# Repricing a planner's reductions and narrow matmuls, and splitting one weight blob a stage earlier, in a decoder layer

## The chip, the cores and the metric

The kernel runs on one core of one Trainium2 chip. The metric is device microseconds of one execution, from the runtime's measurement around the program; the profile's span, from the first to the last instruction, is 1.8 us shorter. A core has TensorE (PE: matmuls, with its weight loads PEld), VectorE (DVE), ScalarE (ACT), GpSimd (POOL) and SyncE (SP, which here only issues loads). Each runs its own instructions in the order in which they are written.

## The reference

One layer of a hybrid decoder for 512 tokens of width 2048, all in float32. Cut to what matters here:

```python
mod = silu(c) @ W_ada + b_ada            # shift1, scale1, gate1, shift2, scale2, gate2
h   = modulate(rms_norm(x), shift1, scale1)
u   = h @ W_in                           # conv group | 8 query heads | k, v of 3 branches | gates
y_conv = B * causal_conv3(C * H)         # 1024 channels
y_nsa  = attention(...)                  # 8 heads of 128, 2 kv heads; blocks of 128 queries
x   = x + gate1 * ([rms_norm(y_conv) | rms_norm(y_nsa)] @ W_out)
h   = modulate(rms_norm(x), shift2, scale2)
x   = x + gate2 * (relu(h @ W1) ** 2 @ W2)
out = rms_norm(x)
```

For each block of 128 queries, attention has a compressed branch (32 columns of pooled keys), a selected branch and a sliding-window branch. With 512 tokens every block of keys is selected, so that the last two are plain causal softmax over the keys so far. The three results are weighted by sigmoid gates and added.

## The kernel before

Matmuls keep float32's precision by splitting each operand into a high half and a low half (both F32R) and adding three products: high by high, high by low, low by high (`mm3`). A weight blob of 128 x 1024 is loaded by SP into a buffer `raw` (three of them, numbered 115 to 117 here), ScalarE rounds it to the high half, and VectorE subtracts to get the low half (`weights`). Both halves lie in a pair named `wh` in the profile (two pairs, 113 and 114).

The kernel has three stages, each recorded in full and then ordered by a planner (`Order`) before anything is issued:

- the front stage: the adaLN products (`wa`, dotted with silu(c) on VectorE into `late` and summed into `mod`), the projections of h (`ps`), compression, convolution, and the convolution half normalised into `mix`;
- the attention stage: for two groups of four heads and four blocks of 128 queries, scores (`s`, three PSUM banks), their maximum (`nm`) on VectorE, the exponential (`p`) on ScalarE, scaling by gate over sum (`cf`), transposes of p through TensorE (`pt`, two banks), the split of each transpose into `tt` (high half ScalarE, low half VectorE) and the product with the values (`pv`); `sr` is the sum of squares at the end of a block. Beside these, out_conv(m), m from 0 to 15, multiplies blob m of `w_oc` by `mix`: 24 matmuls into `pw`, 384 in all, ended by an update of `x` on VectorE. Nothing in attention waits for them; they are what TensorE does while it waits. Four query heads of the second group get their rotary embedding (`rt`, `t`, `q`) here too;
- the feed-forward stage: the attention half of the output projection, then the two large products.

The planner replays a recorded stage with a price for each instruction (`price`: duration, and a lag until its result is seen), a queue for each engine, bandwidth for loads and a count of buffers. At every step it takes the instruction that can start first, and among equals the one with the lower lane number, then the one wanted first. Lanes 0 to 2 order TensorE's work: what has lane 0 (transposes and pv) stands ahead of scores (1) and of out_conv (2). Where TensorE would wait in the replay, it takes the next lane. It makes six passes, each with the last one's times as targets, and keeps the shortest. What comes out is written as the program order of every engine, so that at run time an engine never takes a later instruction first: a price that is wrong is not corrected on the chip.

`with wanted()` gives what is recorded in it a target `SOON` (10 us) ahead of the end of the stage, as against 10 us behind it for work that nothing in the stage needs. Tiles that the next stage reads are kept.

Of the kernel before, what the change touches and what calls it, by code (L numbers as in the profile page):

```python
# [48 lines left out]
class Order:  # L49
# [43 lines left out]
    def price(self, eng, op, out, ins, kw):  # L93

        n = Order.width(out)
        if "dma" in op:
            return (0.42 if eng == "sync" else 0.55), 0.0
        if eng == "tensor":
            if op == "matmul" and ins[0].dtype == F32:
                return max(self.wide[0], n * self.wide[1]), 0.2  # L100
            return (0.109 if op == "transpose" else max(0.06, 0.0015 + n * 0.000453)), 0.2
        if eng == "scalar":
            aps = len(ins) - 1
            more = 0.1 if kw.get("accum_out") is not None else 0.0
            return (0.18 if n < 16 else 0.09 + 0.00084 * n + (0.09 * max(0, aps) if not more else 0.19)), 0.16
        if n < 16:
            return 0.1, 0.14
        if op == "scalar_tensor_tensor":
            return 0.14 + 0.00101 * n, 0.14
        if op in ("tensor_scalar", "tensor_copy", "memset"):  # L110
            return 0.13 + 0.0005 * n, 0.14
        if op == "tensor_reduce":
            n = max(Order.width(x) for x in ins) * (1.7 if n > 16 else 1)
        return 0.068 + 0.00104 * n, 0.14

    def record(self, eng, op, real, args, kw):
# [159 lines left out]
def hybrid_layer(ctx: ExitStack, tc: tile.TileContext, a, out):  # L276
# [91 lines left out]
    def weights(src, cols=1024, spare=False):  # L368
        raw = next(wraw)[:, :cols]
        nc.sync.dma_start(out=raw, in_=src)  # L370
        wh, wl = (slot(F32R, name="sw") for _ in range(2)) if spare else next(whl)
        wh, wl = wh[:, :cols], wl[:, :cols]
        nc.scalar.activation(wh, raw, AF.Copy)
        nc.vector.tensor_tensor(out=wl, in0=raw, in1=wh.bitcast(F32), op=OP.subtract)
        return wh, wl
# [123 lines left out]
    def scale_col(which, k, sc, g, n=1):  # L499
        nc.vector.scalar_tensor_tensor(out=aff[:, which * NK + k:which * NK + k + n],  # L500
                                       in0=mod[:, sc * NK + k:sc * NK + k + n], scalar=1.0,
                                       in1=vec[:, g + k:g + k + n], op0=OP.add, op1=OP.mult)
# [145 lines left out]
    for s, (name, k) in enumerate(steps[:-1]):  # L648
        grp = 0 if name == "w_kv" else 1
        first, last = (grp, k) in begins, (grp, k) in finals  # L650
        if first:
            ps = [bank() for _ in range(8)]
        wh, wl = w
# [168 lines left out]
    for j in range(8):  # L822
# [4 lines left out]
        for i in range(3):  # L827
            n = 3 * j + i
# [30 lines left out]
    for g in range(NG):  # L859
        pv = [bank() for _ in range(NQ)]  # L860
        for blk in range(4):
            wh, wl = weights(a["w_v"][g * 4 + blk], BLOB)
# [49 lines left out]
    for g in range(NG):  # L912
        pq = [bank() for _ in range(NR)]
        order_k = range(NK) if g < NG - 1 else range(NK - 1, -1, -1)
        for at, k in enumerate(order_k):
            if at % 2 == 0:
                wh, wl = weights(a["w_q"][g * 8 + k // 2])
# [13 lines left out]
        tick()  # L931
    more_ada(len(todo))
    scale_col(1, 0, M_SC2, V_N2, NK)
    for t in [rot] + qs + raws + kwin + list(vv.values()) + mix:
        order.keep(t)
    order.emit()
# [25 lines left out]
    def out_conv(m):  # L962
        if m % 2 == 0:
            x1.append(pair(name="x1"))
            order.keep(x1[-1])
            nc.sync.dma_start(out=x1[-1], in_=a["xt"][m // 2])
        ps = next(pws)
        wh, wl = weights(a["w_oc"][m])
        with lane(2):
            for k in range(8):  # L970
                s = slice(k * P, (k + 1) * P)
                mm3(ps, wh[:, s], wl[:, s], mix[k][:, 0], mix[k][:, 1], k == 0, k == 7)
        x = x1[m // 2][:, m % 2]
        nc.vector.scalar_tensor_tensor(out=x, in0=ps, scalar=col(M_G1, m), in1=x, op0=OP.mult, op1=OP.add)
# [90 lines left out]
    m = 2  # L1065
# [111 lines left out]
    for k in range(8):  # L1177
        wh, wl = oa[k] if k < 2 else hilo(hl_tile(), raw_blob(a["w_oa"][k]))
# [315 lines left out]
    for f in range(8):  # L1494
# [7 lines left out]
        for q in range(3 if last else 4):  # L1502
            raw = [raw_blob(a["w_f2"][4 * f + q, b]) for b in range(4)]
            ps = [{}, {}]
            for i, w in enumerate(operands(raw, 4 * f + q)):
# [3 lines left out]
                for j in range(2):  # L1509
                    mp = 2 * q + j  # L1510
                    m = 2 * mp
# [119 lines left out]
```

## Time and profile before

| what | value |
|---|---|
| three runs | 2114.53, 2115.92, 2116.34 us (median 2115.92) |
| the profiled execution | 2115.59 us, span 2113.8 us |
| busy share of the span | PE 98%, weight loads 91%, DVE 89%, ACT 48%, POOL 6% |
| granted TensorE clock, mean | 0.993 |
| attention stage | 554.25 to 759.2 us |
| maxima of scores (nm) | 64, on 128 to 512 columns |
| DMA | 454 MB, 215 GB/s |

A line of the profile's groups gives engine, operation, the tile written and those read, shapes and count, then busy time and mean duration in ns, then the engine's idle time just ahead and who ended it. All recorded operations have one line of code, 122, that of the planner's record; so rows are told apart by their tiles. A line of the order in time gives start, duration, engine, operation and count; matmuls are pipelined, so their durations overlap, and what one costs is read from the starts of a run of them.

### The profile page before, as it was taken

The numbers are of one execution on the slowest core, as the hardware profiler recorded it, in microseconds if no ns is written. First come the engines' busy times: TensorE is split into PE (matmuls) and PEld (weight loads), VectorE is DVE, ScalarE is ACT, GpSimd is POOL, SyncE is SP. The second block draws the span as 40 slices with busy tenths as digits, with TensorE's granted clock in tenths as the row PEclk, the third lists the DMA queues.
The fourth block names the chain that finished last, engine by engine and source line by source line (L and its number), as shares of the span: only waits on it lengthen the run. The fifth ranks groups of instructions, "written<-read, shape, count | busy, mean of one in ns | idle before, by whom it ended". The sixth has DMA issues, their size and how long they took to land.

```text
span 2113.8 us, 38166 instructions
## 1 busy us (share of the span) xinstructions
PE 2068.4 (98%) x15070; PEld 1923.7 (91%) x15070; DVE 1885.7 (89%) x3039; ACT 1007.3 (48%) x1471; POOL 128.2 (6%) x244
## 2 busy tenths in 40 slices
PE   8999999999999999999999999999999999999997
PEld 6888787898777779999999999999999999999997
DVE  7999888888987556999999999999899999999997
ACT  5432433222455434766666666666444333334354
POOL 0000000000000001022211112111000000000000
PEclk8999999999999999999999999999999999999998
DMA  8897588888321144467666676668976466476442
GB/s 335 340 340 249 181 297 325 315 288 311 138 80 41 51 141 154 135 215 225 210 204 207 207 217 200 208 206 288 332 268 211 167 242 220 145 255 237 150 172 90
DMA packets 144130, 454.17 MB, mean 215 GB/s; under 512 B 15824, under 2 KB 20176, under 8 KB 143952
## 3 DMA queue, kind: packets, MB, share of 16 engines
q1 hardware_dynamic: 108816, 386.72, 53.0%
q0 software_dynamic: 34048, 63.98, 9.6%
q8 instruction: 118, 1.93, 0.4%
q10 hardware_dynamic: 1088, 1.05, 0.1%
q14 instruction: 60, 0.49, 0.1%
HBM read 383.53 MB, written 68.16 MB: 214 GB/s over the span
## 4 chain that ended last, share of the span: by engine, by line
PE 72%; DVE 9%; DMA 4%; ACT 2%; issue 2%; DVEq 0%; POOL 0%; SPq 0%; ACTq 0%
PE pf L122 55%; PE ps L122 11%; PE pw L122 3%; DMA rw<-in_w_f 1%; PE pv L122 1%; DVE hl L122 1%; DVE t L122 1%; DVE x L122 1%; PE s L122 1%; DMA wa<-in_w_ada 1%; PE pt L122 1%; DMA raw<-in_cmp_w 1%; DVE nm L122 1%; DVE wh L122 1%; DMA tk<-g 1%
## 5 line engine op out<-in xcount | busy, mean ns | idle before, releaser
L122 PE MATMUL pf<-tk,hl 128*128 128x256 f32 x10704 | 1223.3, 277 | 3.0 <-DVE hl L122 2.2
L122 PEld LDWEIGHTS pf<-tk,hl 128*128 128x128 f32 x10704 | 1219.9, 188 | 5.3 <-DVE hl L122 3.5
L122 ACT ACTIVATE hl<-rw 128x1024 fp32r<-128x1024 f32 x269 | 285.5, 1062 | 324.9 <-PE pf L122 280.1
L122 DVE TENSOR_TENSOR hl<-rw,hl 128x1024 fp32r<-128x1024 f32 (+2 forms) x351 | 336.5, 968 | 29.4 <-ACT hl L122 29.2
L122 ACT ACTIVATE hl<-sg 128x1024 fp32r<-128x1024 f32 x180 | 191.1, 1062 | 220.3 <-PE pf L122 172.8
L122 PE MATMUL ps<-h_m,wh 128*128 128x512 f32 x1080 | 252.0, 390 | 0.0
L122 DVE SCALAR_TENSOR_TENSOR t<-wa,cs 128x1024 bf16<-128x1024 f32 x192 | 234.5, 1221 | 16.1 <-DMA wa<-in_w_ada 13.8
L122 PEld LDWEIGHTS ps<-h_m,wh 128*128 128x128 f32 x1080 | 201.1, 188 | 41.5 <-DVE wh L122 0.3
L122 ACT ACTIVATE wh<-raw 128x1024 fp32r<-128x1024 f32 (+1 forms) x106 | 112.7, 1063 | 243.8 <-PE ps L122 215.7
L122 DVE TENSOR_TENSOR hl<-sg,hl 128x1024 fp32r<-128x1024 f32 (+2 forms) x193 | 188.1, 986 | 25.3 <-ACT hl L122 25.3
L122 PE MATMUL ps<-h,wh 128*128 128x512 f32 x840 | 198.7, 392 | 3.4 <-ACT h L122 2.3
L122 PEld LDWEIGHTS ps<-h,wh 128*128 128x128 f32 x840 | 157.7, 189 | 37.0 <-ACT h L122 2.7
L122 DVE TENSOR_TENSOR wh<-raw,wh 128x1024 fp32r<-128x1024 f32 (+1 forms) x106 | 129.9, 1225 | 21.2 <-ACT wh L122 19.9
L122 DVE TENSOR_TENSOR sg<-sg,rw 128x1024 f32<-128x1024 f32 x120 | 146.1, 1217 | 0.2
L122 DVE SCALAR_TENSOR_TENSOR x<-pf,mod,x 128x256 f32<-128x256 f32 (+1 forms) x280 | 131.8, 485 | 14.5 <-PE pf L122 12.8
L122 POOL DMA_DIRECT2D g<-gt x192 | 101.2, 532 | 379.7 <-ACT hl L122 222.1
L122 PE MATMUL pw<-mix,wh 128*128 128x512 f32 x384 | 109.7, 405 | 0.0
L122 DVE TENSOR_TENSOR sg<-rw 128x1024 f32<-128x1024 f32 x60 | 73.2, 1220 | 16.7 <-DMA rw<-in_w_f 14.0
L122 ACT ACTIVATE t<-t 128x512 f32<-128x512 f32 (+3 forms) x131 | 74.9, 572 | 21.1 <-DVE t L122 18.8
L122 PEld LDWEIGHTS pw<-mix,wh 128*128 128x128 f32 x384 | 69.6, 190 | 11.0 <-issue 0.5
L122 DVE TENSOR_TENSOR rw<-rw 128x1024 f32<-128x1024 f32 x60 | 73.0, 1217 | 0.0
L122 ACT ACTIVATE gt<-t 128x512 fp32r<-128x512 f32 x96 | 60.3, 630 | 22.6 <-DVE t L122 17.7
(215 smaller groups left out, 1802.1 us busy)
## 6 DMA issues: line engine op xcount, KB each, us to landing
rw<-in_w_f SPq DMA_DIRECT2D x263, 512.0 KB, 3.9
wa<-in_w_ada SPq DMA_DIRECT2D x192, 512.0 KB, 6.0
tk<-g SPq DMA_DIRECT2D x114, 512.0 KB, 6.2
g<-gt POOLq DMA_DIRECT2D x192, 256.0 KB, 4.1
raw<-in_w_conv SPq DMA_DIRECT2D x32, 512.0 KB, 4.3
x<-in_xt SPq DMA_DIRECT2D x16, 512.0 KB, 7.2
raw<-in_w_kv SPq DMA_DIRECT2D x16, 512.0 KB, 4.4
raw<-in_w_cv SPq DMA_DIRECT2D x16, 512.0 KB, 4.5
```

The costliest lines, as they stand in the source:

```text
L122: x.i, x.eng, x.call = len(self.nodes), eng, (lambda: real(*args, **kw))
```

## The change

Two edits. In `price`: a reduction on VectorE (`tensor_reduce`) is priced by the columns that it reads, also where it writes fewer than 16; before, such a one fell under the rule for small outputs, 0.1 us. A maximum over 512 scores goes from 0.1 to 0.60 us in the plan, one over 128 from 0.1 to 0.20. A matmul of F32R operands costs at least 0.1 us in the plan instead of 0.06; this touches those of 32, 128 and 160 columns, all of them scores or their masks. In `hybrid_layer`: the first blob of `w_oc` is loaded and split at the end of the front stage, as wanted, and out_conv(0) uses it.

```diff
         if eng == "tensor":
             if op == "matmul" and ins[0].dtype == F32:
                 return max(self.wide[0], n * self.wide[1]), 0.2
-            return (0.109 if op == "transpose" else max(0.06, 0.0015 + n * 0.000453)), 0.2
+            return (0.109 if op == "transpose" else max(0.1, 0.0015 + n * 0.000453)), 0.2
...
+        if op == "tensor_reduce":
+            rows = max(Order.width(x) for x in ins)
+            return 0.068 + 0.00104 * rows * (1.7 if n > 16 else 1), 0.14
         if n < 16:
             return 0.1, 0.14
...
-        if op == "tensor_reduce":
-            n = max(Order.width(x) for x in ins) * (1.7 if n > 16 else 1)
         return 0.068 + 0.00104 * n, 0.14
...
     scale_col(1, 0, M_SC2, V_N2, NK)
+    with wanted():
+        first = [weights(a["w_oc"][0])]
     for t in [rot] + qs + raws + kwin + list(vv.values()) + mix:
         order.keep(t)
     order.emit()
...
         ps = next(pws)
-        wh, wl = weights(a["w_oc"][m])
+        wh, wl = first.pop() if first else weights(a["w_oc"][m])
         with lane(2):
```

Every engine has the same instructions before and after; what differs is their order. The feed-forward stage keeps its order, and so does the front stage, but for the moved blob. In attention most of the order is new. Rows before have L122, rows after L123 (three lines more).

First place: TensorE where attention begins, behind the third group of scores (`kslc`: the selected branch with its compressed columns, `kwin`: the window, `vec`: the identity of the transposes). Before:

```order
L122 MATMUL s<-kslc_108,q 128x160 x2
L122 MATMUL s<-kwin,q 128x128
L122 MATMUL s<-mask_r,ident_r 128x128
L122 MATMUL s<-kwin,q 128x128 x3
L122 MATMUL s<-mask_r,ident_r 128x128
L122 MATMUL s<-kwin,q 128x128 x3
L122 MATMUL s<-mask_r,ident_r 128x128
L122 MATMUL s<-kwin,q 128x128 x2
L122 MATMUL pt<-vec,p 128x128 x2
L122 MATMUL pw<-mix,wh 128x512
```

These begin with the fourth group's last two; up to the first pair of transposes there is no `pw`. After, from the third group on:

```order
L123 MATMUL s<-kslc_108,q 128x160 x2
L123 MATMUL pw<-mix,wh 128x512 x3
L123 MATMUL s<-kslc_108,q 128x160
L123 MATMUL s<-mask_r,ident_r 128x128
L123 MATMUL s<-kslc_108,q 128x160 x2
L123 MATMUL pw<-mix,wh 128x512 x2
L123 MATMUL s<-kwin,q 128x128
L123 MATMUL s<-mask_r,ident_r 128x128
L123 MATMUL s<-kwin,q 128x128 x3
L123 MATMUL s<-mask_r,ident_r 128x128
L123 MATMUL s<-kwin,q 128x128 x2
L123 MATMUL pw<-mix,wh 128x512 x2
```

Out_conv's matmuls have moved between the scores: 3, 2, 2, and then (not shown) 4 and 1 ahead of the first transpose. Up to the end of the first block (its `sr`) 35 of the 384 stand now, 20 before; up to the second's 54 and 47; behind the row norm's broadcast at the end of attention (`pt<-t,ones`) 70 and 77.

Second place: VectorE at the end of the front stage, where the adaLN dots end and `mod` is summed. Before:

```order
L122 TENSOR_TENSOR wh_114<-raw_116,wh_114 128x1024
L122 SCALAR_TENSOR_TENSOR t_101,late_138<-wa_133,cs_127 128x1024
L122 SCALAR_TENSOR_TENSOR t_101,late_138<-wa_130,cs_126 128x1024
L122 SCALAR_TENSOR_TENSOR t_101,late_138<-wa_131,cs_127 128x1024
L122 SCALAR_TENSOR_TENSOR t_101,late_138<-wa_132,cs_126 128x1024
L122 SCALAR_TENSOR_TENSOR t_101,late_138<-wa_133,cs_127 128x1024
L122 TENSOR_TENSOR mod_124<-late_138 128x16
```

And after:

```order
L123 TENSOR_TENSOR wh_114<-raw_116,wh_114 128x1024
L123 SCALAR_TENSOR_TENSOR t_101,late_138<-wa_133,cs_127 128x1024
L123 SCALAR_TENSOR_TENSOR t_101,late_138<-wa_130,cs_126 128x1024
L123 TENSOR_TENSOR wh_113<-raw_117,wh_113 128x1024
L123 SCALAR_TENSOR_TENSOR t_101,late_138<-wa_131,cs_127 128x1024
L123 SCALAR_TENSOR_TENSOR t_101,late_138<-wa_132,cs_126 128x1024
L123 SCALAR_TENSOR_TENSOR t_101,late_138<-wa_133,cs_127 128x1024
L123 TENSOR_TENSOR mod_124<-late_138 128x16
```

The blob's low half has moved three dots ahead of the sum. On ScalarE its high half (wh_113 from raw_117) stands behind that of wh_114 and ahead of the four copies of `ps`; on SP its load stands four adaLN loads earlier, behind that of the last blob of w_q and one adaLN load.

Third place: VectorE in the third block of the first group, from the split of the compressed branch's transpose to that of the window's first one. Before:

```order
L122 TENSOR_TENSOR tt_3987<-pt_3975,tt_3987 128x512
L122 TENSOR_REDUCE nm_3993<-s_3972 128x1
L122 TENSOR_SCALAR p_3978<-p_3978,cf_4000 128x512
L122 TENSOR_REDUCE nm_3993<-s_3973 128x1
L122 TENSOR_SCALAR p_3979<-p_3979,cf_4000 128x512
L122 TENSOR_SCALAR p_3980<-p_3980,cf_4000 128x512
L122 TENSOR_REDUCE nm_3993<-s_3971 128x1
L122 TENSOR_TENSOR tt_3985<-pt_3974,tt_3985 128x512
```

And after:

```order
L123 TENSOR_TENSOR tt_3990<-pt_3978,tt_3990 128x512
L123 TENSOR_REDUCE nm_3996<-s_3975 128x1
L123 TENSOR_REDUCE nm_3996<-s_3976 128x1
L123 RECIPROCAL cf_4003<-sm_3999 128x4
L123 MEMSET pc_3991 128x96
L123 TENSOR_TENSOR cf_4003<-cf_4003,gates_241 128x4
L123 TENSOR_SCALAR p_3980<-p_3980,cf_4003 128x512
L123 TENSOR_TENSOR tt_3988<-pt_3977,tt_3988 128x512
```

The third maximum and two of the scalings of the next block now stand behind the split. On TensorE, between the first of the three `pv` matmuls that read this `tt` and the other two, which need VectorE's half, three `pw` stand instead of two. The rotary pieces of the second group have moved later: 10 of the 20 stand ahead of the second block's `sr`, where 15 did.

## The prediction

> **What bounds the kernel now.** I read the page first, then the busy time by stages, then the waits of TensorE, then the order of time at the one place where they pile up. TensorE bounds nearly everywhere:
>
> ```profile
> span 2113.8 us, 38166 instructions
> ...
> PE 2068.4 (98%) x15070; PEld 1923.7 (91%) x15070; DVE 1885.7 (89%) x3039; ACT 1007.3 (48%) x1471; POOL 128.2 (6%) x244
> ```
>
> The change can act only in the attention stage, 554.25 us (first score matmul) to 759.2 us (last out-projection matmul of the conv half); the order before 554 us differs in one moved blob, and the order of the feed-forward stage is the same instruction for instruction. The next rows (stretch, then busy us of PE, PEld, DVE, ACT, POOL, then TensorE's granted clock) show the stage, and five neighbouring stretches at its start:
>
> ```profile
> 554.25:600.00 45.75, 41.48 (x216) 33.33 (x215) 41.72 (x126) 26.02 (x78) 0.00 (x0) 0.93 0.24 86
> 554.25:759.20 204.95, 197.38 (x1019) 156.40 (x1018) 156.83 (x381) 101.37 (x258) 0.00 (x0) 0.98 0.20 66
> ...
> 553.09:556.51 3.42, 2.63 (x18) 2.24 (x16) 2.68 (x10) 1.80 (x3) 0.00 (x0) 1.00 1.02 413
> 556.51:559.92 3.41, 2.32 (x16) 2.01 (x16) 3.30 (x12) 2.31 (x9) 0.00 (x0) 1.00 0.62 253
> 559.92:563.33 3.41, 2.67 (x12) 2.34 (x11) 2.75 (x10) 2.01 (x8) 0.00 (x0) 0.50 0.03 7
> 563.33:566.75 3.42, 3.42 (x14) 3.14 (x13) 2.79 (x10) 2.73 (x8) 0.00 (x0) 0.50 0.49 153
> 566.75:570.16 3.41, 3.41 (x24) 3.15 (x24) 3.02 (x12) 1.02 (x5) 0.00 (x0) 1.00 0.11 13
> ```
>
> Two losses are to be seen. TensorE is idle for 204.95 - 197.38 = 7.6 us of the stage, and from 559.92 to 566.75 us it runs at half clock. All that the stage loses by name is in TensorE's own list of waits (total us, times, longest):
>
> ```profile
> PE pv L122 <- DVE tt L122: 4.3, 8, 0.7
> PE s L122 <- ACT p L122: 1.8, 2, 1.4
> PE pt L122 <- DVE p L122: 0.7, 1, 0.7
> PE pt L122 <- DVE sr L122: 0.2, 1, 0.2
> ```
>
> That is 7.0 us. The three waits of the second and third row, 2.5 us, stand in the first block of attention, just ahead of the half clock (start, duration, count, and in brackets the idle time before and its releaser):
>
> ```profile
> 554.77 0.27 PE L122 MATMUL s<-mask_r,ident_r 128*128 128x128 f32 x1
> ...
> 555.32 0.40 PE L122 MATMUL s<-kslc,q 128*128 128x160 f32 x2
> 557.07 0.34 PE L122 MATMUL s<-kslc,q 128*128 128x160 f32 x1 [1.35 <-ACT p L122]
> ...
> 558.17 0.33 PE L122 MATMUL s<-kwin,q 128*128 128x128 f32 x1 [0.42 <-ACT p L122]
> ...
> 560.79 0.69 PE L122 MATMUL pt<-vec,p 128*128 128x128 f32 x2 [0.74 <-DVE p L122]
> 561.14 0.78 PE L122 MATMUL pw<-mix,wh 128*128 128x512 f32 x1
> ...
> 741.32 18.06 PE L122 MATMUL pw<-mix,wh 128*128 128x512 f32 x77
> ```
>
> TensorE fills its three score banks by 555.7 us and then has nothing: no out-projection matmul (pw) stands in its order until 561.14 us, since in the old plan the first blob of w_oc is split only then. (The last row, from the end of the stage, gives the price of a pw in a dense run: 18.06 / 77 = 0.235 us.)
>
> **The change, part by part.** *What the new prices tell the planner.* Measured reductions against what they were priced at:
>
> ```profile
> L122 DVE TENSOR_REDUCE nm<-s 128x1 f32<-128x512 f32 x16 | 11.0, 685 | 1.2 <-PE s L122 1.2
> ...
> L122 DVE TENSOR_REDUCE nm<-s 128x1 f32<-128x128 f32 x16 | 4.2, 280 | 0.9 <-PE s L122 0.8
> ```
>
> The old rule gave 0.1 us to each; the new one gives 0.068 + 0.00104 x 512 = 0.60 and 0.20. Over 64 maxima (16 of each width, prices 0.20, 0.33, 0.47, 0.60) that is 16 x 1.2 = 19 us of VectorE's 156.8 us that the old plan did not see. So it planned VectorE early where it was late. The price of narrow matmuls (0.06 to 0.10) moves toward what the trace shows: from 554.77 us the mask matmul and the three narrow ones after it run to the next mask at one per 0.11 us. No instruction is added or removed on any engine; all is order.
>
> *Term 1, the first block.* The new order puts pw matmuls between the scores: 3 after the third score, then 2, 2, 4 and 1, twelve ahead of the first transposes (the order shown above, first place). Of the 1.35 us wait, 3 x 0.235 = 0.7 is filled; the rest stays, because the fourth score needs the first maximum and its exponential, and these do not come sooner:
>
> ```profile
> 535.02 1.22 DVE L122 TENSOR_TENSOR wh<-raw,wh 128x1024 fp32r<-128x1024 f32 x1
> ...
> 548.73 1.23 DVE L122 SCALAR_TENSOR_TENSOR t<-wa,cs 128x1024 bf16<-128x1024 f32 x1
> ...
> 553.76 1.23 DVE L122 SCALAR_TENSOR_TENSOR t<-wa,cs 128x1024 bf16<-128x1024 f32 x1 [1.26 <-DMA wa<-in_w_ada]
> ...
> 555.55 0.63 DVE L122 TENSOR_TENSOR rt<-qr,rot 128x512 f32<-128x512 f32 x1
> 556.09 0.28 DVE L122 TENSOR_REDUCE nm<-s 128x1 f32<-128x128 f32 x1
> ...
> 556.38 0.68 DVE L122 TENSOR_TENSOR rt<-qr,rot 128x512 f32<-128x512 f32 x1
> ...
> 556.56 0.37 ACT L122 ACTIVATE p<-s,nm 128x128 f32<-128x128 f32 x1 [1.51 <-DVE pc L122]
> ```
>
> VectorE's queue up to that maximum (adaLN dots, then one rope piece at 555.55, then the maximum at 556.09) is the same in both orders. The 0.42 us is covered by two pw (0.47). The 0.74 us goes, since the transposes now stand behind twelve pw and a ninth group of scores; a split of the second blob (1.22 us) stands ahead of the four scalings on VectorE in the new order, which I allow 0.2 us. Left: 0.65 + 0.25 = 0.9 of 2.5 us. Gain 1.6 (bounds 0.7, if only the first wait shrinks, and 2.5).
>
> *Term 2, the clock.* In the half-clock stretch TensorE was busy 2.67 + 3.42 = 6.09 us; at full clock that work takes half. Gain 3.05 if the clock is kept, 0 if not. The stretch ahead of the drop was 68% busy (2.32 of 3.41); the one before that, 77% (2.63 of 3.42), kept the clock. With at most 0.75 us idle the new first stretch is 78% or more, and its filling is 512 columns wide. So I take 3.05.
>
> The Trainium skill, "TensorE: Matmul & The Clock Gate", section "Part 1: The HAM clock gate (the "warmup" mystery)", has the clock halved after an idle window of about 3.4 us, and under "HAM oscillation" warns only of gaps beyond that. The trace agrees with the window's length (half clock for 6.83 us, twice 3.41) but not with the condition, since the longest gap here was 1.35 us. By that rule these gaps are not what decides, and the sum would be 3.05 us less; that is the first rival.
>
> *Term 3, the later waits,* 4.3 + 0.2 = 4.5 us, nine of them, each where a pair of pv matmuls waits for VectorE's half of a split transpose (tt). The one at 616.58 us:
>
> ```profile
> 614.26 0.60 ACT L122 ACTIVATE tt<-pt 128x512 fp32r<-128x512 f32 x1 [2.36 <-PE pt L122]
> ...
> 615.24 0.68 DVE L122 TENSOR_REDUCE nm<-s 128x1 f32<-128x512 f32 x1
> 615.84 0.68 DVE L122 TENSOR_TENSOR tt<-pt,tt 128x512 fp32r<-128x512 f32 x1
> ...
> 616.58 0.73 PE L122 MATMUL pv<-tt,vv 128*128 128x512 f32 x2 [0.67 <-DVE tt L122]
> ```
>
> ScalarE's half is done at 614.86, but the split stands in VectorE's queue behind three maxima, planned at 0.1 us each and taking 0.6. In the new order (third place above) two maxima and one scaling (and three operations on four or 96 columns) stand between it and the split ahead of it, where three and three stood, and TensorE has three pw instead of two ahead of the pair: at least the one maximum, 0.6 us, less queue and 0.23 us more cover, against 0.67. I read the other places only by their pw counts, so I take just over half: gain 2.5. Bounds: +4.5, and -1.0, two new waits of about 0.5 from the heavier rope work behind the second block.
>
> *Term 4, the blob moved into the front stage.* Its load is one place in SP's queue ahead of four adaLN loads and waits for its buffer until VectorE's split of 535.02 us ends, 536.2; the load behind it feeds the dot at 548.73 or later, 12 us on. ScalarE's half has to wait until TensorE frees the operand buffer, one blob (24 matmuls, 5.6 us at 0.23) before 554.25, at 548.7, and then comes ahead of ScalarE's bank copies, which wait for the last matmul. VectorE's 1.22 us comes after the dot of 548.73 and pushes two dots into the 1.26 us that VectorE now waits for a load at 553.76. Cost 0; if that cover is gone (the load lands sooner) VectorE still ends no later than now; if it lands later, up to 1.2. In attention the same blob is one split less.
>
> *Term 5, the tail.* After the row norm's broadcast (pt<-t,ones) 77 pw remain now (741.32, above), 70 in the new order:
>
> ```profile
> 740.86 1.02 PE L122 MATMUL pt<-t,ones 128*128 128x512 f32 x2
> ...
> 759.22 1.07 PE L122 MATMUL pf<-mixa,wh 128*128 128x512 f32 x4
> ...
> 742.55 0.75 DVE L122 SCALAR_TENSOR_TENSOR ya<-ya,vec,sacc 128x512 f32<-128x512 f32 x1 [2.09 <-ACT sacc L122]
> ...
> 756.92 1.21 DVE L122 TENSOR_TENSOR wh<-raw,wh 128x1024 fp32r<-128x1024 f32 x1
> ```
>
> VectorE works from 742.55 to 758.1 on what the next stage needs, 17.3 us after the broadcast; 70 pw and the broadcast give 0.46 + 16.4 = 16.9. The new order has one blob split less to do after its normalising begins (1.2 us), so it fits by about 0.8. Cost 0, at worst 1.
>
> *Sum.* -1.6 - 3.05 - 2.5 = -7.15 us. Behind 759 us all follows TensorE, so it stays to the end. The profiled execution took 2115.59 us (0.3 below the median 2115.92): 2108.4 us. 0.2% of it, 4.2 us, is about what a measurement of this kernel can tell from no change.
>
> **The rivals.** *The clock falls anyway* (13%). For: 78% busy against 77% that kept it is a thin margin, and where a stretch begins is not the kernel's to choose; the maxima at the start still come late. Against: twelve wide matmuls where there were none. Then 2108.4 + 3.05 = 2111.5.
>
> *VectorE becomes the bound of the first 45 us* (12%). It is busy 41.72 of 45.75 us there, so it has 4.0 us to give, and the new order wants every step about 4.65 us sooner. Against: 10 instead of 15 of the rope instructions (0.68 us each) stand ahead of the second block's end, 3.4 us deferred. If it holds, terms 1 and 2 give 4.0 and term 3 nothing: 2111.6.
>
> *Slower: the split transposes come late everywhere* (5%). 48 tt splits on VectorE each gate a pair of pv; TensorE's order is fixed, so a wait there cannot be filled. Nine wait now. The gain is gone when the 48 wait 0.15 us more on average (7.15 / 48), and it is slower by 0.2% from 0.24; at 0.3 us the time is 2108.4 + 14.4 = 2122.8. For: ropes of the second head group are pushed into the third block. Against: VectorE idles 204.95 - 156.83 = 48 us in the stage.
>
> **How the numbers follow.** The forecast holds 70%, with 2105.5 (all three terms at their better bound: 2.5 + 3.05 + 4.5 = 10.05) to 2111.5 as its own range. The two rivals on this side lie at 2111.5 and 2111.6, the bound of term 3 with a little of terms 4 and 5 adds 1.5: 2105.2 to 2113 for eight in ten. Below 2111.7 (0.2% under the median) lie nearly all of the first 70% and a little under a third of each of the two rivals: faster 74%, same 21%, slower 5%.
>
> **What would show it.** Right: granted clock 1.00 throughout 554 to 570 us; first wait of the stage near 0.65 us and the next ones under 0.3; pv's waits on tt at about 2 us in all; the attention stage near 198 us long; the feed-forward stage as long as now. Wrong: half clock after 558 us; a later start of attention than 554.3; pv waiting on tt over 5 us; VectorE without a gap up to 600 us while TensorE waits; a wait ahead of the first pf matmul.

## The result, and the profile after

The changed kernel takes 2105.67 us (median of 8 runs, 2100.70 to 2111.30) against 2116.93 us before (8 runs, 2110.08 to 2120.42): a ratio of 0.9948, 95% interval 0.9930 to 0.9966, or 11.0 us less (7.2 to 14.8). Two more series of the same kernel, below, gave 0.9938 (0.9916 to 0.9960) and 0.9936 (0.9923 to 0.9949). The forecast was 2108.4, range 2105.2 to 2113.0.

The profiled execution took 2100.70 us, the shortest of its series; the one of before, 2115.59, was 1.3 below that series' median. So the two profiles lie 14.9 us apart, 3.6 more than the medians. By place: the first score matmul starts at 553.47 instead of 554.25 (-0.78), the attention stage (first score to first `pf`) is 191.31 us long instead of 204.97 (-13.66), and all behind it is 0.46 us shorter. The earlier start is no effect of the change that two profiles could show: in the later profiles of the changed kernel, below, the first score matmul starts at 554.40 and 554.08. The page:

```profile
span 2098.9 us, 38151 instructions
...
PE 2059.4 (98%) x15070; PEld 1920.7 (92%) x15070; DVE 1885.0 (90%) x3039; ACT 1007.0 (48%) x1471; POOL 128.2 (6%) x244
```

The stretches that answer to those of before (length, then busy us of PE, PEld, DVE, ACT, POOL, then the granted clock):

```profile
553.47:744.78 191.31, 189.77 (x1020) 154.54 (x1018) 155.87 (x380) 99.98 (x258) 0.00 (x0) 1.00 0.20 69
553.47:599.22 45.75, 44.21 (x254) 36.49 (x253) 44.34 (x132) 25.32 (x78) 0.00 (x0) 1.00 0.25 90
...
559.92:566.75 6.83, 6.83 (x45) 6.00 (x44) 6.80 (x27) 4.23 (x15) 0.00 (x0) 1.00 0.25 80
```

The clock is 1.00 throughout: where TensorE issued 12 + 14 matmuls at half clock before, it issues 45. TensorE's idle time in the stage falls from 7.6 to 1.54 us. Its list of waits (total us, times, longest) is down to two rows:

```profile
PE s L123 <- ACT p L123: 1.3, 1, 1.3
PE pv L123 <- DVE tt L123: 0.3, 1, 0.3
```

7.57 - 1.54 = 6.0 us of idle time and 3.05 us of half clock make 9.1, not the 13.66 that the stage lost. The rest is in the waits of TensorE's weight loads, a list that the prediction did not use. Before, the four largest:

```profile
PEld pv L122 <- DVE tt L122: 14.0, 33, 1.1
PEld pv L122 <- ACT tt L122: 6.1, 26, 0.4
PEld s L122 <- ACT p L122: 3.0, 7, 1.5
PEld pt L122 <- DVE sr L122: 2.4, 6, 0.6
```

And after:

```profile
PEld pv L123 <- ACT tt L123: 5.4, 25, 0.3
PEld pv L123 <- DVE tt L123: 3.9, 17, 0.6
PEld s L123 <- ACT p L123: 2.6, 5, 1.7
PEld pt L123 <- DVE sr L123: 1.0, 5, 0.3
```

A pair of pv waited for VectorE's half of a split 33 times, where the matmul rows show 8. One of the others, before, at 589.90 us; TensorE's order first, then the weight load of the same pair:

```profile
589.07 0.86 PE L122 MATMUL pw<-mix,wh 128*128 128x512 f32 x3
589.90 0.74 PE L122 MATMUL pv<-tt,vcmp 128*128 128x512 f32 x2
590.48 0.60 PE L122 MATMUL pt<-vec,p 128*128 128x128 f32 x4
```

```profile
589.90 0.30 PEld L122 LDWEIGHTS pv<-tt,vcmp 128*128 128x128 f32 x2 [0.41 <-DVE tt L122]
```

The three pw before the pair cost 3 x 0.235 = 0.70 in a dense run and took 0.83 here, the pair 0.58 instead of 0.47: 0.24 us lost, with no idle time in the matmul rows, since their modelled ends reach to the next start. The load's 0.41 shows the place, but is not the price either, because a load may lie idle while the matmul before it still runs.

The starts of the matmul rows give a price, as an estimate from the traces: the time from one start to the next at full clock, less the lower quartile of such times, over all kernels here, for matmuls as wide as the first of the two. Summed over the stage, what TensorE lost just ahead of pv matmuls by this account is 10.2 us before and 2.2 after (9.7 and 1.7 with the median in place of the quartile). So 8.0 of the 13.66 us lie where the split transposes are waited for.

### The profile page after: what moved, and what is told of

Same layout as the page of the kernel before. It is cut to its first block, busy times and chain, and to the rows that moved or that the text cites. A ratio compares the mean times of both kernels' runs of the same rounds, so it can differ in the third digit from the quotient of the medians.

```text
span 2098.9 us, 38151 instructions
## 1 busy us (share of the span) xinstructions
PE 2059.4 (98%) x15070; PEld 1920.7 (92%) x15070; DVE 1885.0 (90%) x3039; ACT 1007.0 (48%) x1471; POOL 128.2 (6%) x244
## 4 chain that ended last, share of the span: by engine, by line
PE 76%; DVE 7%; DMA 2%; ACT 2%; issue 1%; DVEq 0%; POOL 0%; SPq 0%; ACTq 0%
PE pf L123 56%; PE ps L123 12%; PE pw L123 4%; DVE t L123 2%; PE pv L123 2%; PE s L123 1%; DVE hl L123 1%; PE pt L123 1%; DVE x L123 1%; DVE tk L123 1%; DMA raw<-in_cmp_w 1%; DMA wa<-in_w_ada 0%; DVE wh L123 0%; DMA g<-gt 0%; DMA rw<-in_w_f 0%
## 5 line engine op out<-in xcount | busy, mean ns | idle before, releaser
L123 PE MATMUL pf<-tk,hl 128*128 128x256 f32 x10704 | 1221.8, 277 | 4.1 <-DVE hl L123 2.8
L123 PEld LDWEIGHTS pf<-tk,hl 128*128 128x128 f32 x10704 | 1218.5, 188 | 6.3 <-DVE hl L123 3.6
L123 ACT ACTIVATE hl<-rw 128x1024 fp32r<-128x1024 f32 x269 | 285.5, 1062 | 324.8 <-PE pf L123 286.7
L123 DVE TENSOR_TENSOR hl<-rw,hl 128x1024 fp32r<-128x1024 f32 (+2 forms) x351 | 335.9, 967 | 30.2 <-ACT hl L123 30.0
L123 ACT ACTIVATE hl<-sg 128x1024 fp32r<-128x1024 f32 x180 | 191.1, 1062 | 222.8 <-PE pf L123 176.8
L123 PE MATMUL ps<-h_m,wh 128*128 128x512 f32 x1080 | 251.9, 390 | 0.0
L123 DVE SCALAR_TENSOR_TENSOR t<-wa,cs 128x1024 bf16<-128x1024 f32 x192 | 234.2, 1220 | 17.9 <-DMA wa<-in_w_ada 15.5
L123 PEld LDWEIGHTS ps<-h_m,wh 128*128 128x128 f32 x1080 | 201.3, 188 | 41.2
L123 ACT ACTIVATE wh<-raw 128x1024 fp32r<-128x1024 f32 (+1 forms) x106 | 112.6, 1062 | 252.9 <-PE ps L123 225.3
L123 DVE TENSOR_TENSOR hl<-sg,hl 128x1024 fp32r<-128x1024 f32 (+2 forms) x193 | 187.8, 985 | 27.5 <-ACT hl L123 27.3
L123 PE MATMUL ps<-h,wh 128*128 128x512 f32 x840 | 198.7, 393 | 3.4 <-ACT h L123 2.3
L123 PEld LDWEIGHTS ps<-h,wh 128*128 128x128 f32 x840 | 157.8, 189 | 37.4 <-ACT h L123 2.7
L123 DVE TENSOR_TENSOR wh<-raw,wh 128x1024 fp32r<-128x1024 f32 (+1 forms) x106 | 129.8, 1225 | 20.9 <-ACT wh L123 18.3
L123 DVE TENSOR_TENSOR sg<-sg,rw 128x1024 f32<-128x1024 f32 x120 | 145.9, 1216 | 0.2
L123 DVE SCALAR_TENSOR_TENSOR x<-pf,mod,x 128x256 f32<-128x256 f32 (+1 forms) x280 | 131.6, 483 | 14.4 <-PE pf L123 12.7
L123 POOL DMA_DIRECT2D g<-gt x192 | 101.2, 532 | 377.6 <-ACT hl L123 250.2
L123 PE MATMUL pw<-mix,wh 128*128 128x512 f32 x384 | 109.3, 404 | 0.0
L123 ACT ACTIVATE t<-t 128x512 f32<-128x512 f32 (+3 forms) x131 | 74.8, 571 | 20.9 <-DVE t L123 18.7
L123 DVE TENSOR_TENSOR sg<-rw 128x1024 f32<-128x1024 f32 x60 | 73.0, 1217 | 11.4 <-DMA rw<-in_w_f 9.2
L123 PEld LDWEIGHTS pw<-mix,wh 128*128 128x128 f32 x384 | 69.1, 189 | 11.3 <-issue 0.5
L123 DVE TENSOR_TENSOR rw<-rw 128x1024 f32<-128x1024 f32 x60 | 72.9, 1215 | 0.0
L123 ACT ACTIVATE gt<-t 128x512 fp32r<-128x512 f32 x96 | 60.3, 630 | 19.7 <-DVE t L123 14.5
```

The source lines that it names most:

```text
L123: x.i, x.eng, x.call = len(self.nodes), eng, (lambda: real(*args, **kw))
```

## The experiments

The theory (A): the three edits act in different places. The price of the maxima takes away the waits on the split transposes, all through the stage; the early blob fills the start and keeps the clock; the floor for narrow matmuls does little. Its rivals: the early blob brings nearly all (B); any new order would have (C); the clock has nothing to do with the filling (D); the floor does nothing at all (E).

**The price of the maxima alone.**

```diff
+        if op == "tensor_reduce":
+            rows = max(Order.width(x) for x in ins)
+            return 0.068 + 0.00104 * rows * (1.7 if n > 16 else 1), 0.14
         if n < 16:
             return 0.1, 0.14
...
-        if op == "tensor_reduce":
-            n = max(Order.width(x) for x in ins) * (1.7 if n > 16 else 1)
```

> Kernel before with the price of the maxima alone (no early blob, narrow matmuls at 0.06 as before). Theory A (two parts with places of their own): the price of the maxima takes away the waits of pv's weight loads on VectorE's half of a split transpose (14.0 us before, 3.9 after the whole change), so here at most 6 us of them; the start is left as it was, with no pw ahead of the first transposes: some 7 us of half clock again and 2 us or more of waits there. In this order only 58 pw stand behind the row norm's broadcast (70 after, 77 before): 0.46 + 58 x 0.235 = 14.1 us against 16 to 17 of VectorE, so 2 to 3 us of wait may appear ahead of the first pf. Attention 196 to 200 us against 205 before and 191.3 after. Rival B (the early blob brings nearly all): 203 us or more, with 11 us or more of those weight-load waits. Rival C (any new order would have brought it): waits gone at the start too, 191 to 194 us.

2109.86 us, ratio 0.9963 (0.9952 to 0.9975). Its stage, the stretch at half clock, and its weight-load waits:

```profile
557.09:752.71 195.62, 192.81 (x1020) 158.80 (x1018) 156.09 (x381) 102.19 (x259) 0.00 (x0) 0.98 0.21 71
561.52:568.35 6.83, 6.83 (x28) 6.45 (x29) 5.87 (x20) 4.99 (x16) 0.00 (x0) 0.50 0.19 59
```

```profile
PEld pv L123 <- DVE tt L123: 3.1, 14, 0.5
```

This is as theory A had it; the stage is even 0.4 us below the 196 expected, with a shorter wait in the tail than expected (0.3 us ahead of the first pf and 0.3 ahead of the third, where 2 to 3 were expected). The start is no better than before (2.2 us of waits, 6.83 us at half clock) and the stage is 204.97 - 195.62 = 9.35 us shorter all the same. B and C fall.

**The early blob alone.**

```diff
+    with wanted():
+        first = [weights(a["w_oc"][0])]
...
-        wh, wl = weights(a["w_oc"][m])
+        wh, wl = first.pop() if first else weights(a["w_oc"][m])
```

> Kernel before with the early blob of w_oc alone (both prices as before). Theory A: the start is cured (full clock between 554 and 570 us, waits on p below 1.5 us), the waits of pv's weight loads on VectorE's tt stay at 10 us or more; 58 pw behind the broadcast, so 0 to 3 us of wait ahead of the first pf. Attention 199 to 203 us. Rival B (the blob brings nearly all): 191 to 194 us. Rival D (the half clock had nothing to do with the filling): a stretch of half clock in the first 20 us of attention again, and 203 us or more.

2113.81 us, 0.9982 (0.9970 to 0.9994), but the profiled execution shows no cure of the start:

```profile
554.14:759.49 205.35, 198.31 (x1019) 157.10 (x1018) 156.03 (x382) 101.19 (x258) 0.00 (x0) 0.98 0.20 67
558.20:568.44 10.24, 9.51 (x33) 8.16 (x33) 7.31 (x25) 4.76 (x17) 0.00 (x0) 0.50 0.30 115
```

Four pw stand ahead of the fourth group of scores, and TensorE still waits 2.37 us there, then runs 10.24 us at half clock. So A fails at the start. The stage is as long as D had it, but with 2.37 us of wait left this is no test of D. The weight-load waits on tt stay (11.2 us), as A had it. What makes the median 0.2% shorter is not to be seen in this profile, whose stage is 0.4 us longer than before's.

**All but the early blob** (both prices).

> The whole change without the early blob. Theory A: as the price of the maxima alone at the start (half clock and 2 us or more of waits), weight-load waits on VectorE's tt at most 6 us, and no wait ahead of the first pf, since 75 pw stand behind the broadcast (18.1 us): 195 to 198 us in attention, so the floor for narrow matmuls is worth the tail's 2 to 3 us and little else. Rival B: 203 us or more. Rival E (the floor does nothing, 75 or 58 pw in the tail are the same): within 0.7 us of the price of the maxima alone, and no wait ahead of pf in either.

2108.21 us, 0.9954 (0.9939 to 0.9970); stage 195.37 us with a wait of 2.80 us and half clock at the start, weight-load waits on tt 2.6 us, no wait ahead of pf. The start and the waits are as A had them; but the floor brings 0.25 us of stage over the maxima alone, not the 2 to 3 of theory A; that is E's number.

**All but the floor** (maxima and blob).

> The whole change without the floor of 0.1 us for narrow matmuls. Theory A: start cured and weight-load waits on VectorE's tt at most 6 us, as after the whole change, but only 46 pw behind the broadcast: 0.46 + 46 x 0.235 = 11.3 us against 15.6 to 17 of VectorE, so 4 to 6 us of wait ahead of the first pf: 194 to 198 us in attention against 191.3. Rival E (the floor does nothing): 190.5 to 192 us and no wait ahead of pf.

2107.01 us, 0.9947 (0.9928 to 0.9965); stage 196.43 us. Again the start is not cured (2.59 us of wait, 6.8 us at half clock). The tail is where the floor counts in this profile: 46 pw are left behind the broadcast, and they don't cover VectorE. The waits there are 2.26 us, where 4 to 6 were expected, and half clock follows them too, for 3.41 us from 750.74.

```profile
736.13 1.02 PE L123 MATMUL pt<-t,ones 128*128 128x512 f32 x2
736.59 11.03 PE L123 MATMUL pw<-mix,wh 128*128 128x512 f32 x46
748.89 0.70 PE L123 MATMUL pf<-mixa,wh 128*128 128x512 f32 x2 [1.27 <-DVE x L123]
750.59 12.34 PE L123 MATMUL pf<-mixa,wh 128*128 128x512 f32 x46 [0.99 <-DVE wh L123]
```

**The changed kernel again.** VectorE's rows at the start gave a new theory (F): the first maximum stands behind the adaLN dots, and the last dot waits for its load, so TensorE's first wait is a race between that load and TensorE's own arrival at attention; the out_conv matmuls that the blob makes possible there cover a part.

> The changed kernel once more, for a second profile of its start. In the profiles of five kernels so far the first maximum of attention comes 1.8 to 2.4 us after VectorE's last adaLN dot begins, and that dot waited for its load (0.4 us in the changed kernel's first profile, 0.7 to 1.8 in the four partial ones and 1.26 before); the four partial ones, two of them with the early blob, all show half clock in the 20 us behind it. Theory F (a race: the first score bank comes free when the last adaLN load lands, and TensorE reaches attention by its own clock; the early blob covers only some 0.7 to 1.2 us of it): this profile may fall either way; with 2 us or more of wait ahead of the fourth group of scores it shows half clock and an attention stage of 194 to 196 us, with 1.3 us or less full clock and 190.5 to 192. Theory A (the early blob always keeps the clock): full clock and 190.5 to 192 us whatever the wait.

2102.72 us, 0.9938. The wait was 0.76 us, the clock 1.00 and the stage 190.80 us, which A and F both allow; the third profile of this kernel, below, parts them.

**Two dots moved out of the way.**

```diff
+LEFT, AFTER = 1, 2
...
-    more_ada(len(todo))
+    more_ada(len(todo) - LEFT)
...
+    def last_ada():
+        while todo:
+            n = todo.pop(0)
+            acc = halves_of(n)
+            for i in range(2):
+                w = slot(name="wa")[:, :1024]
+                nc.sync.dma_start(out=w, in_=a["w_ada"][2 * n + i])
+                nc.vector.scalar_tensor_tensor(out=temp(name="scr").bitcast(BF16), in0=w, scalar=1.0,
+                                               in1=cs[i].rearrange("p a b -> p (a b)"),
+                                               op0=OP.mult, op1=OP.mult, accum_out=acc[i])
+            bias_in(n, acc)
...
             if g == 0:
                 head(NR + qb)
+            if g == 0 and qb == AFTER:
+                last_ada()
```

(`cs` is kept for the attention stage too.)

> The changed kernel with the last two adaLN dots (the last of 96 columns, first needed at the end of the kernel) and the sum behind them moved from the end of the front stage into the third block of attention, with loads of their own there. Theory F: VectorE has 2.5 + 0.35 us less ahead of the first maximum and one load less to wait for, so the wait ahead of the fourth group of scores falls to 0.5 us or less, the clock stays at 1.00, attention takes 189 to 191.5 us in spite of 2.5 us more VectorE work, and the time is 1 to 4 us below the changed kernel's. Rival G (the load that is now the last lands as late, the wires being full at some 400 GB/s there): wait of 1.2 us or more, as likely half clock, no gain. Rival H (VectorE, 44.3 us busy of the first 45.75, is the bound there): the first wait goes, and waits of pv on VectorE's tt of 1.5 us or more come in the third block.

2100.44 us, 0.9929 (0.9911 to 0.9947). No row of TensorE's own list of waits is left in the stage; what remains are weight-load waits, the three largest:

```profile
554.57:744.57 190.00, 189.96 (x1020) 155.47 (x1018) 156.71 (x384) 100.63 (x258) 0.00 (x0) 1.00 0.21 72
```

```profile
PEld pv L124 <- ACT tt L124: 5.5, 24, 0.3
PEld pv L124 <- DVE tt L124: 2.2, 11, 0.3
PEld s L124 <- ACT p L124: 1.7, 7, 0.4
```

The fourth group of scores starts 0.88 us after the three pw do, so these three run straight into it. Theory F holds. The wait did not stay (rival G), and no wait of pv on VectorE came in its place (rival H).

**Filling without reordering.** The kernel before, with eight matmuls of no use ahead of the first block's waits: five, one and two.

```diff
...
+    padding = {(1, 3): 5, (2, 0): 1}
...
+    def fillers(n):
+        order.pad[len(order.nodes)] = [
+            lambda: tc.nc.tensor.matmul(spare, ident_r, kslc[0][:, 0, 32:], start=True, stop=True)] * n
...
+                if g == 0 and qb == 0 and (b, r) in padding:
+                    fillers(padding[b, r])
...
+                if (g, qb, b, kb) == (0, 0, 1, 0):
+                    fillers(2)
```

> Kernel before with eight matmuls added whose results nobody reads (512 wide, into out_conv's idle bank): five ahead of the fourth group of scores, one ahead of the first window scores, two ahead of the first transposes; no other change. It tells filling from reordering. Clock theory: TensorE is 1.9 us busier in the first block's waits, so where before idled 2.5 us and then ran at half clock (559.92 to 566.75), this keeps 1.00 if no wait above 1.3 us is left, and attention takes 201 to 203 us against 205. If VectorE's last adaLN load lands late (a wait of 2 us or more remains), half clock comes all the same, 204 to 206 us. Rival (gaps do not decide the clock): half clock with no wait above 1.3 us left.

2117.72 us, 1.0004 (0.9993 to 1.0015): no gain. VectorE's last dot waited 1.61 us for its load in this profile, the fourth group 1.52 us behind the five fillers, and half clock followed:

```profile
555.89 1.37 PE L971 MATMUL pw<-kslc,ident_r 128*128 128x512 f32 x5
558.79 0.34 PE L123 MATMUL s<-kslc,q 128*128 128x160 f32 x1 [1.52 <-ACT p L123]
```

Half clock was expected with 2 us of wait left, full clock with 1.3 or less; it came with 1.5. The stage took 207.15 us, above the 204 to 206 expected for half clock: the fillers are some 1.9 us of work (8 x 0.235), and a wait of 0.94 us stands ahead of the first pf.

**More cover ahead of the fourth group.** The planner holds VectorE busy for the stage's first 1.4 us.

```diff
+        free["vector"] = self.lead
...
+    order.more, order.lead = 0.0, 1.4
```

> The changed kernel, with the planner told that VectorE is 1.4 us late when attention begins, so that five out_conv matmuls stand ahead of the fourth group of scores instead of three. Theory F: 0.47 us more of that wait is filled; of 1.26 us (first profile of the changed kernel) some 0.8 is left, the clock stays at 1.00 more often, and the time is 0 to 2 us below the changed kernel's; the tail has 78 out_conv matmuls instead of 70. Rival: nothing, as the matmuls taken there are missing later in the first blocks (28 ahead of the first block's end instead of 35), and the waits of pv's weight loads on tt grow by as much.

2106.25 us, 0.9950 (0.9935 to 0.9965): no gain over the changed kernel, where 0 to 2 us were expected. Five pw stand there, the wait was 1.10 us, and the clock fell for 3.41 us, where the changed kernel's first profile kept it with 1.26:

```profile
555.10:747.97 192.87, 191.58 (x1020) 156.41 (x1018) 156.03 (x382) 100.25 (x258) 0.00 (x0) 0.99 0.20 71
557.46:560.87 3.41, 2.31 (x16) 1.81 (x15) 3.04 (x15) 1.91 (x9) 0.00 (x0) 1.00 0.97 390
560.87:564.28 3.41, 3.41 (x13) 2.74 (x12) 3.31 (x13) 2.18 (x8) 0.00 (x0) 0.50 0.17 65
```

**The last four ran on one chip in more rounds.** First the kernel with two dots moved:

> The same kernel as e6_defer, timed in more rounds beside the changed kernel on one chip. Theory F: since it waits for no load at the start, its runs keep the clock there each time and spread less; median 1 to 5 us below the changed kernel's, and a second profile again with full clock, no wait above 0.3 us ahead of the fourth group of scores and an attention stage of 189.5 to 190.5 us. Rival: the gain in the first three rounds was chance, the medians within 1 us.

2100.07 us, 0.9913 (0.9899 to 0.9926); stage 190.03 us at clock 1.00, no wait. Its eight runs of both series have the median 2100.2; seven lie between 2099.6 and 2101.7, the eighth at 2105.0.

The changed kernel:

> The changed kernel, timed in five rounds beside the others: 2101 to 2107 us, and by theory F a spread of 8 us or more, as in its twelve runs so far (2099.2 to 2111.3), since the clock at the start falls in some executions and not in others; this profile may show either (half clock: attention 193 to 196 us; full clock: 190.5 to 191.5).

2105.78 us (2100.77 to 2107.91), 0.9936 (0.9923 to 0.9949); its 17 runs of all series have the median 2104.35, from 2099.2 to 2111.3. This profile shows the other outcome of the race. VectorE, then TensorE, then the stretches:

```profile
555.16 1.23 DVE L123 SCALAR_TENSOR_TENSOR t<-wa,cs 128x1024 bf16<-128x1024 f32 x1 [1.64 <-DMA wa<-in_w_ada]
557.49 0.28 DVE L123 TENSOR_REDUCE nm<-s 128x1 f32<-128x128 f32 x1
```

```profile
558.47 0.34 PE L123 MATMUL s<-kslc,q 128*128 128x160 f32 x1 [2.19 <-ACT p L123]
```

```profile
554.08:749.50 195.42, 192.95 (x1020) 157.48 (x1019) 156.15 (x380) 99.99 (x258) 0.00 (x0) 0.98 0.19 67
...
559.78:566.61 6.83, 6.83 (x26) 6.15 (x27) 4.92 (x19) 2.94 (x11) 0.00 (x0) 0.50 0.27 82
```

So the same kernel spends 4.1 to 4.6 us more in this stage when the load lands late: 3.4 us of clock (6.83 / 2), and 0.9 to 1.4 us of wait.

The race can be read off four profiles that have three pw ahead of the fourth group and the same VectorE queue up to the first maximum. In the changed kernel's three, the last dot starts 0.34 us ahead of the first score matmul, 0.15 behind it and 1.08 behind it; the first wait is 0.76, 1.26 and 2.19 us. In the kernel with blob and floor, below, it is 0.26 ahead and 0.85. Counting a start ahead as negative, the wait is each time 1.10 or 1.11 us more than that distance.

The race is not all of the spread: between the fastest and the slowest of the 17 runs lie 12.1 us, and the three profiles, all of runs below 2105 us, are up to 5.2 apart. What the slower runs lost is not shown.

The floor alone (0.06 becomes 0.1 in the price of matmuls):

> Kernel before with the floor for narrow matmuls alone. Theory A: by itself it does not help: the planner believes in more work of TensorE's own, so it puts fewer out_conv matmuls between (18 ahead of the first block's end instead of 20, 285 instead of 307 ahead of the broadcast), the start has none as before, and the waits of pv's weight loads on VectorE's tt are 14 us or more: attention 205 to 208 us, half clock at the start, time 0 to 4 us above before. Rival (dearer narrow matmuls are the truer price and help alone): attention 203 us or less.

2119.58 us, 1.0005 (0.9996 to 1.0014); stage 207.64 us, weight-load waits on tt 13.8 us, as theory A had it. And blob and floor without the maxima:

> The whole change without the price of the maxima. Theory A: weight-load waits on VectorE's tt of 11 us or more, as with the early blob alone (11.2); no wait ahead of the first pf (76 matmuls in the tail); attention 200 to 206 us by the clock at the start, time 2 to 6 us below before and 6 to 9 above the changed kernel's. Rival B (blob and floor without the maxima bring most): 196 us or less.

2118.84 us, 1.0000 (0.9990 to 1.0009); stage 204.63 us, weight-load waits on tt 12.8 us. Without the price of the maxima, blob and floor together bring nothing that can be measured, where theory A expected 2 to 6 us; its weight-load waits and stage came as expected.

In one table (the ratio to before as timed beside it; in the profiled execution the stage, its time at half clock, and the waits of pv's weight loads on VectorE's tt):

| maxima | blob | floor | ratio | stage us | half clock us | waits us |
|---|---|---|---|---|---|---|
| - | - | - | 1 | 204.97 | 6.8 | 14.0 |
| yes | - | - | 0.9963 | 195.62 | 6.8 | 3.1 |
| - | yes | - | 0.9982 | 205.35 | 10.2 | 11.2 |
| - | - | yes | 1.0005 | 207.64 | 10.2 | 13.8 |
| yes | - | yes | 0.9954 | 195.37 | 6.8 | 2.6 |
| yes | yes | - | 0.9947 | 196.43 | 6.8 | 2.7 |
| - | yes | yes | 1.0000 | 204.63 | 3.4 | 12.8 |
| yes | yes | yes | 0.9948, 0.9938, 0.9936 | 191.31, 190.80, 195.42 | 0, 0, 6.8 | 3.9, 4.0, 4.0 |
| yes, two dots moved | yes | yes | 0.9929, 0.9913 | 190.00, 190.03 | 0, 0 | 2.2, 2.0 |

Wherever the maxima's price is added, the ratio falls by 0.0035 to 0.0064 (7 to 14 us) and the waits by 8 to 11 us. By the account from the starts, what TensorE loses ahead of pv is 7.7 to 10.4 us in the kernels without that price (the one with fillers among them) and 1.5 to 2.6 in all that have it. The blob brings 0.0005 to 0.0018 where the maxima's price is missing, 0.0016 beside it, and 0.0006 to 0.0018 beside both prices; with the floor the ratio changes by +0.0018 to -0.0011. Single steps of that size are within the intervals: that the blob helps on average is likely from its own interval (0.9970 to 0.9994), but how often it keeps the clock is not shown. That the floor helps is not shown either.

## Why the prediction was right, point by point

Sign and size came out: 2105.67 us lies 2.7 us below the forecast and inside the range, near its lower end. The sum of 7.15 us was 4.1 too small for the medians and 7.7 too small for the two profiles, and the miss has one main place.

That the median fell inside the range is in part luck, since two errors pull in opposite ways. With term 3 at the 9.4 us measured and terms 1 and 2 as forecast, the sum is 1.6 + 3.05 + 9.4 = 14.05 us and the time 2101.5, below the range; four of the eight runs lie below 2105.2. What brings the median back is most likely that the start of attention is not cured in every execution, as the third profile shows; for the runs without a profile it is not shown.

*Term 3, the later waits, is the mis-sized term:* 2.5 us forecast, bounds -1.0 to +4.5, about 9.4 measured. In the changed kernel's first profile it is what is left of 13.66 without 3.05 of clock and 1.25 of first waits, 9.4, of which 8.0 lie ahead of pv by the account from the starts and most of the rest ahead of transposes; with the maxima priced alone, and the start as bad as before, the stage lost 9.35. The bound was taken from TensorE's idle time between matmul rows, 4.5 us in nine waits. That list starts to count only when the modelled end of the last matmul has passed. The weight loads waited 14.0 us for the same tile, 33 times, and these waits fell by 10.1 us (those on `sr` by 1.4 and on ScalarE's half by 0.7). The mechanism was the one described: maxima that stand behind the split instead of ahead of it. The sign named for the whole, an attention stage near 198 us, came out as 190.8 and 191.3 where the clock was kept. The Trainium skill, "Perfetto Trace Analysis", section "Identifying the Most-Contended Engine", says that the matmul busy share is not a good measure of how close a kernel is to its roofline, because pipelined matmuls look smaller in the trace, and to use the weight loads' share, with that of peak FLOPs, instead. The traces of this stage agree that the matmul share is a poor guide, though here it hid idle time: it was 96% before, which left 7.6 us, and the stage lost 13.66; the weight loads' share went from 76 to 81%.

*Term 1, the first block:* a gain of 1.6 was forecast, with 0.9 us left. In the first profile 1.26 us were left, all in the first wait (0.65 forecast), so the gain was 1.25; the other two waits are gone, not merely short. In the two later profiles 0.76 and 2.19 us were left. The step that failed is the one that took the first maximum's time from one execution as fixed: VectorE's queue up to it is the same, but its last load is not.

*Term 2, the clock:* the 3.05 us came in two of three profiles of the changed kernel, and not in the third. (Of the kernel before there is one profile, so how often it loses the clock is not known.) The rival "the clock falls anyway", given 13%, is therefore something that happens in some executions of the changed kernel and not in others; half clock after 558 us was also named ahead as a sign of being wrong. The rival's reason was half right: the stretch was less full than thought (38% busy in the third profile, 556.37 to 559.78), because the load was late. The rule of the Trainium skill that was weighed there ("TensorE: Matmul & The Clock Gate", "Part 1: The HAM clock gate (the "warmup" mystery)", half clock behind an idle window of about 3.4 us) is met in the window's length again: half clock came for 3.4, 6.8 or 10.2 us. In its condition the runs disagree: the clock fell with longest gaps of 0.85 to 2.80 us, and TensorE never stood still for 3.4. Another section of that page, which the prediction did not weigh, "A second HAM failure mode: psum-queue depth-cycling", tells of a kernel in which frequent short idle times between groups of matmuls were enough for it. The ten drops seen here agree in that no gap reached 3.4 us, but in most of them it was one or two gaps and not many.

*Term 4, the blob in the front stage,* was right at 0 for the part that VectorE does. Whether the load that stands a place earlier makes the last adaLN load later cannot be told: that dot waited 1.26 us before the change, and 0 to 1.64 after it.

*Term 5, the tail,* was right. 70 pw cover VectorE, and no wait stands ahead of the first pf:

```profile
728.47 16.47 PE L123 MATMUL pw<-mix,wh 128*128 128x512 f32 x70
744.78 11.04 PE L123 MATMUL pf<-mixa,wh 128*128 128x512 f32 x48
```

That it is tight was right too: with 58 left the kernel with the maxima alone waits 0.3 + 0.3 us, and with 46 the one without the floor 1.27 + 0.99.

*VectorE as the bound of the first 45 us* (12%) was near: it is busy for 44.34 of 45.75 us. With two dots fewer ahead (40.3 of 45.75 in the kernel with the dots moved), TensorE has no idle time there. Split transposes that come late everywhere (5%) were not seen.

## What to carry to other kernels

A planner that writes a fixed order pays for a price that is too low at each place where the underpriced instruction stands ahead of one that another engine waits for; 0.1 for a maximum of 0.3 to 0.7 us cost about 8 us of 2117 here, and the price alone, three lines, gave most of the gain. Read the waits of the weight loads beside those of the matmuls: the weight loads' list overstated what came out here (12.2 us less for 9.4), the matmuls' list understated it, and a bound from the matmuls' list alone, 4.5, was half of it. Before a wait is filled, see what the releasing engine itself waits for: moving two dots that nobody needed yet was worth another 2 to 6 us of the median, and seven of its eight runs lie within 2.1 us, while more filling in front of the same wait brought nothing that could be measured.

## What the hardware showed beyond that

The clock fell without any long pause. At the start of attention it fell in ten of the fourteen profiles. In the 3.41 us ahead of each drop TensorE was 19 to 78% busy by its rows, with no gap above 2.80 us. Half clock then lasted one, two or three stretches of 3.41 us. In seven of the ten TensorE was busy all through the first of these (3.38 us or more of 3.41); two of the seven were back at full clock behind it, and five ran a second one at half clock. No busy share decides it: a stretch with 78% lost the clock, in the kernel with blob and floor,

```profile
556.02:559.43 3.41, 2.67 (x18) 2.16 (x19) 3.33 (x13) 2.04 (x9) 0.00 (x0) 1.00 0.62 251
559.43:562.84 3.41, 3.41 (x11) 2.54 (x11) 3.39 (x12) 2.41 (x9) 0.00 (x0) 0.50 0.02 7
```

while one with 77% kept it before the change (553.09 to 556.51) and one with 69% in the kernel without the floor (552.76 to 556.18). Its condition stays open. What was seen without exception is that the clock stayed at 1.00 in the three profiles with a first wait of 0.76 us or less and no other in the first block (the changed kernel's second, and both with the dots moved), and fell in all eight with 1.35 us or more; in the three between these it went either way.

The start of attention is not the only place. A drop to half clock also begins between 230.7 and 237.5 us in eight of the fourteen profiles, and between 1510.7 and 1529.4 us in six, each but one lasting 3.41 us (the other 6.83); the changed kernel's third profile has a drop at 235.56 us, and its first two have none there. So two executions of one kernel can differ by such a stretch in other stages as well.
